# Splitting the attention values and probabilities: three float32r products per block in place of a native float32 one

## The chip, the cores and the metric

The kernel runs on one NeuronCore of a Trainium2 chip. The metric is the device time of one execution in microseconds; lower is better. Of the core's engines, PE is TensorE (matrix products), ACT is ScalarE, DVE is VectorE, POOL is GpSimd and SP is the queue that issues the transfers.

## The reference, cut to what matters

One layer of a decoder for 256 positions, all inputs and outputs float32. The part that the change touches is the attention of `nsa_attention`: eight heads in two groups, with a compressed, a selected and a window branch, each weighted by a gate:

```python
p_c = masked_softmax(s_c, mask_c)
o_c = jnp.einsum('bghqn,bngd->bqghd', p_c, vc)
...
p_s = masked_softmax(s_s, mask_s)
o_s = jnp.einsum('bghqm,bgqmd->bqghd', p_s, v_sel)
...
p_w = masked_softmax(s_w, mask_w)
o_w = jnp.einsum('bghqk,bkgd->bqghd', p_w, vwb)
return gbf[..., 0:1] * o_c + gbf[..., 1:2] * o_s + gbf[..., 2:3] * o_w
```

At 256 positions the selection takes every block, so the selected and the window branch are two causal attentions over all keys, w = 0 and 1, of different keys and values. Beside the attention runs an mLSTM of four heads, whose result `h` is normalised and gated; both branches are projected (`w_br`), merged by sigmoid gates of a projection `w_mg`, projected again, and followed by a gated MLP.

## The kernel before, in words

Weights stream in from HBM as float32 tiles `w`, issued on SP. For each weight tile ACT casts a high half `wh` to float32r (L154) and DVE subtracts a low half `wl` = `w` - `wh` (L157); a product of float32 accuracy then takes three float32r products (high by high, low by high, high by low). The helper `mm` (L112) issues them all. The moving operand is read through `turns`, which takes the two halves of its columns in turns. Four buffers hold `wh`, four `wl`, seven `w`. Where a text says fill, it means one `w_mg` tile: one `w`, `wh` and `wl`, and 12 products of 128x512 into `ps_mg`. DVE also multiplies rows of the adaLN weights with the conditioning vector (L276, "ada product"), 128x1024 each, which a ticker hands out one per weight tile. DVE's work thus comes in pairs of a `wl` and an ada product.

The stage in question lies at about 320 to 430 us. PE's order is written out by hand there, inside `tc.manual_schedule`; the order on ACT and DVE is set by the tile scheduler from the program's order, its dependencies and its own priorities, and each engine then works through its list in order. What the hand order says, in short (g is the group, t the half of the positions):

- `ml_weights` and `ml_num` make the mLSTM's numerators (`num`) from the values `mv1` that lie in `projA` behind the attention's values.
- `probs(g, t)` (`nsa_probs`) makes the probabilities: scores on PE, maxima on DVE, exponentials on ACT, then the gates over the sums (L987, L988), and the multiplication with them on DVE (L995) and ACT (L1003).
- `outs(g, t)` (`nsa_out`) goes over the blocks: t = 0 has two, t = 1 four, each 128 keys of one branch, and last the compressed one of 48 rows. For each block PE turns the probabilities of four heads over (L1019, into `ps_pT`), ACT copies them to `pT` (L947), and the block's product into `ps_y` follows one block later (`late`), with a fill between. At the end ACT and DVE split `ps_y` into the halves of `y_nsaT` (L1033, L1034).
- `ml_norm` normalises `num` beside outs(1, 0): DVE makes `vr` and `rs`, ACT does a square root (L205) and eight activations (L1083), DVE eight multiplications (L1085). `ml_outs` turns `num` over beside outs(1, 1) into `y_mlT` (L1097, L1098).
- Behind the last fill ACT takes eight sigmoids of `gates0` (L1171), and the products of `w_br` with `y_mlT` and `y_nsaT` begin (`ps_br`).

The window and selected products are native float32 (one instruction each, two records in the trace); the compressed one is float32r, since its values `vcm` and its `pT` already are. `behind(a, b)` makes the scheduler put a behind b on their engine, with no wait.

Of the kernel before, what the change touches and what calls it, by code (L numbers as in the profile page):

```python
# [14 lines left out]
P = 128  # L15
# [33 lines left out]
YA = 2  # L49
SLOW = (19,21,)  # L50
AHEAD, AHEADMOD, FIRST2 = {6: (11, 12), 7: (13,), 8: (15,), 9: (16,)}, 15, 3
ACOLS = 2596
AW = 392
A_MO, A_G, A_IF, A_V, A_MV = 0, 1024, 1048, 1056, 1568

# [25 lines left out]
def build(ctx: ExitStack, tc: tile.TileContext, d, out, dbg=None):  # L81
# [39 lines left out]
    def t2(shape, name, dt=F32):  # L121
        return p0.tile(shape, dt, name=name, tag="t2", bufs=NT2)
# [455 lines left out]
    KT = pa.tile([P, G, 2, 2, P], F32, name="KT")  # L578
    MV1 = MDV + 1
    projA = pa.tile([P, 2, ACOLS], F32, name="projA")  # L580
    mv1 = projA[:, :, A_MV:].rearrange("p t (h v) -> p t h v", v=MV1)
    nc.vector.memset(mv1[:, :, :, MDV:], 1.0)

    def conv():
# [205 lines left out]
    for gi, kn in enumerate(GROUPS):  # L790
        nxt = gi < len(GROUPS) - 1
        if nxt:
            for ks in STEPS[gi]:
                tk.add(ada_mod(k0 + kn + ks[0], k0 + kn + ks[-1] + 1))
        rate = None
        comp = []

        def work():
            if comp and next(comp[0], 1) is None:
                return  # L800
            comp.clear()
            pace = next(r for n, r in PACE if tiles[0] <= n)
            tk.tick((rate or pace) if nxt or c < 3 else GR2)
            if ring:
                tk.flush()

        c = 0
        first, lag = {}, []

        def catch_up():  # L810
            for args in lag:
                mm(*args)
            lag.clear()

        for b, ks in order_b(gi):
            j = b // 2
            if j not in psb:
                psb[j] = bank(psa if j < HELD else psm, "ps_b")
            ps = psb[j]
            whole = j < HELD  # L820
            shared = j < HELD + 4
            for k in ks:
                need(k0 + k)
                wh, wl = next(wb)
                o = ps[:, (b % 2) * S:(b % 2 + 1) * S]
                opening = k == 0 and (not shared or b % 2 == 0 and (not whole or gi == 0))
                new = first.setdefault(k, tiles[0]) == tiles[0]
                if tiles[0] <= 5:
                    continue
                end = k == kn - 1 and (not shared or b % 2 == 1 and not (whole and nxt))  # L830
                if not new:
                    catch_up()
                    mm_b(o, wh, wl, 0, hT, k0 + k, opening, end)
                else:
                    mm(o, wh, turns(hT[:, k0 + k, 0, :]), opening, False)
                    mm(o, wl, turns(hT[:, k0 + k, 0, :]), False, False)
                    lag.append((o, wh, turns(hT[:, k0 + k, 1, :]), False, end))
            if b % 2 == 1 and ks[-1] == kn - 1 and not (whole and nxt):
                catch_up()
                del psb[j]  # L840
                dst, src = dest_b(b // 2), ps.rearrange("p (a k t) -> p a t k", a=2, t=2)
                if gi == 0:
                    moved.append(lambda dst=dst, src=src: nc.scalar.copy(dst, src))
                elif whole:
                    nc.scalar.copy(dst, src)
                else:
                    ins = nc.vector.tensor_add(dst, src, dst)
                    if gi == 1 and b in SLOW:
                        slow.append(ins)
                if not nxt and b == 3:  # L850
                    ring.clear()
                    rate = GR1
                    comp.append(compress())
                    tk.add(ada_cols(3, 2, 0, KD))
                if not nxt and b == NBLK - 1:
                    conv()
        for c in range(6):
            pss = [bank(psm, "ps_a%d" % t) for t in range(2)]
            aw = AW if c < 4 else 512
            for k in range(k0, k0 + kn):  # L860
                need(k)
                wh, wl = next(wa if c < 4 else wv)
                if k or c:
                    for t in range(2):
                        mm_a(pss[t][:, :aw], hT, k, t, wh, wl, k == k0, k == k0 + kn - 1)
                else:
                    for x, w in ((0, wh), (1, wh), (0, wl)):
                        for t in range(2):
                            mm(pss[t][:, :aw], hT[:, k, x, t * P:(t + 1) * P], turns(w), not x and w is wh, False)
                if not nxt and c in (3, 4) and (k - k0) % 3 == 2:  # L870
                    next(steps)
            for t in range(2):
                dst, src = projA[:, t, c * AW:(c + 1) * AW], pss[t][:, :aw]
                if c >= 4:
                    dst = mv1[:, t, 2 * c - 8:2 * c - 6, :MDV]
                    src = src.rearrange("p (h v) -> p h v", v=MDV)
                if gi == 0:
                    moved.append(lambda dst=dst, src=src: nc.scalar.copy(dst, src))
                else:
                    nc.vector.tensor_add(dst, src, dst)  # L880
            if not nxt:
                if c == 2:
                    while comp:
                        work()
                    Pk = pa.tile([P, 16, 48], F32R, name="Pk", tag="c4")
                    nTr = pa.tile([36, 384], F32R, name="nTr", tag="xe")
                    steps = gate_steps(Pk, nTr)
                    next(steps)
        k0 += kn
# [42 lines left out]
    def fill(n, rate=RATES[0]):  # L932

        for _ in range(n):
            if next(filler, 1) is None:
                tk.tick(rate)


    y_nsaT = pg.tile([P, H, 2, S], F32R, name="y_nsaT", tag="u16")
    y_mlT = p0.tile([P, 8, 2, S], F32R, name="y_mlT", tag="t16")  # L940
    nev = [0]
    marks = {}

# [6 lines left out]
    def nsa_probs(g, t):  # L950
# [53 lines left out]
                                                          scale=l8[:, b, w:w + 1])  # L1004
        return Pt

    def nsa_out(g, t, Pt):
        psy = bank(psa, "ps_y")
        blocks = [(tt, w) for tt in range(t + 1) for w in range(2)] + [None]
        late = None  # L1010
        for i, blk in enumerate(blocks):
            n = P if blk else 48
            ps = bank(psa, "ps_pT")
            for hh in range(HPG):
                if blk is None:
                    src = Pk[:, t * H + g * HPG + hh, :].bitcast(F32)
                else:
                    src = Pt[hh // 2][:, hh % 2, blk[1], :] if t == 0 else Pt[hh][:, blk[0], blk[1], :]
                nc.tensor.transpose(ps[:n, hh * P:(hh + 1) * P], src, ident)  # L1019
            pT = t2([P, 512], "pT", F32 if blk else F32R)  # L1020
            ins = evac(pT[:n], ps[:n])
            if ins is not None:
                marks["last"] = ins
            if late is not None:
                late()
            v = vcm[:, g, :] if blk is None else projA[:, blk[0], A_V + (blk[1] * 2 + g) * P:
                                                       A_V + (blk[1] * 2 + g + 1) * P]
            late = lambda v=v, pT=pT, n=n, i=i: mm(psy, v, pT[:n], i == 0, i == len(blocks) - 1)
            yield
        late()  # L1030
        src = psy.rearrange("p (h k) -> p h k", h=HPG)
        hi = y_nsaT[:, g * HPG:(g + 1) * HPG, 0, t * P:(t + 1) * P]
        nc.scalar.copy(hi, src)  # L1033
        nc.vector.tensor_sub(y_nsaT[:, g * HPG:(g + 1) * HPG, 1, t * P:(t + 1) * P], src, hi)  # L1034


    stm = pa.tile([P, MH, 2, 6], F32, name="stm")
# [17 lines left out]
    def ml_num(h, W):  # L1055
        pn = [bank(psa, "ps_n") for _ in range(2)]
        mm(pn[0][:, :MV1], W[:, 0:P], mv1[:, 0, h], True, True)
        mm(pn[1][:, :MV1], W[:, P:2 * P], mv1[:, 0, h], True, False)
        mm(pn[1][:, :MV1], W[:, 2 * P:3 * P], mv1[:, 1, h], False, True)
        for t in range(2):  # L1060
            nc.scalar.copy(num[:, h, t], pn[t][:, :MDV])
            nc.vector.tensor_copy(den[:, t, h:h + 1], pn[t][:, MDV:MV1])
        for t in range(2):
            nc.vector.bn_stats(stm[:, h, t, :], num[:, h, t, :])
            nc.vector.bn_aggr(mvm[:, h, t, :], stm[:, h, t, :])
# [50 lines left out]
    with tc.manual_schedule(engines={mybir.EngineType.PE}):  # L1116
# [10 lines left out]
        for h in range(MH):  # L1127
            ml_num(h, Ws[h])
            if h % 2:
                fill(h // 2 + 1)  # L1130
        probs(0, 1)
        fill(3)
        outs(0, 0)
# [7 lines left out]
        outs(1, 0, norm)  # L1141
        run_all(norm)
        fill(2)
        outs(1, 1, ml_outs())
        fill(1)
        fill(8 * (NU0 + NU1))
# [651 lines left out]
```

## Time and profile before

| what | value |
|---|---|
| median of 3 runs | 1371.25 us (1370.47 to 1371.87) |
| the profiled execution | 1370.62 us |
| its span | 1368.8 us |
| granted TensorE clock | 1.00 |
| busy PE / DVE / ACT | 1349.4 / 1088.0 / 731.7 us |

The span runs from the first to the last instruction; the time of an execution has 1.8 us more. The lines of the profile stand in the prediction where they are used. In a row of the timeline come the start in us, the busy time, the engine, line and operation, the tiles written and read, and in brackets how long the engine sat idle before it and what ended that. In the chain come start, length and the instructions; a row of one tile's instructions has the shortest, middle and longest duration in ns.

### The profile page before, as it was taken

Reading aid. Unit: us, or ns where it says so; the run is one execution under the profiler, and the core shown is the slowest. Engines: PE = TensorE matmul, PEld = TensorE weight load, DVE = VectorE, ACT = ScalarE, POOL = GpSimd, SP = SyncE. Lnnn points to the kernel's source line nnn. Section 1 sums busy time; section 2 is a strip of 40 time slices with the busy share of each in tenths; the row PEclk is TensorE's granted clock in tenths of the full one; section 3 lists DMA queues with packets and bytes.
Section 4 is the critical chain, followed back from the end, with each engine's and each line's share of the span. In section 5 each row is a group of like instructions: output and inputs, shape, how many; then the busy total and the mean of one; then the engine's idle time right before and its main releaser. Section 6 shows DMA issues by size and latency. Waiting matters only on the chain.

```text
span 1368.8 us, 20928 instructions
## 1 busy us (share of the span) xinstructions
PE 1349.4 (99%) x7862; PEld 1203.5 (88%) x7862; DVE 1088.0 (79%) x1643; ACT 731.7 (53%) x1050; POOL 3.6 (0%) x11
## 2 busy tenths in 40 slices
PE   7999999999999999999999999999999999999998
PEld 6999998888778888889799999988889999998887
DVE  8899978998787897779899889865557667676568
ACT  7654455556576444445765555553345555555342
POOL 0000000000000000000000000000000000000000
PEclk9999999999999999999999999999999999999999
DMA  9999988996877998995389888866666666666662
GB/s 387 418 419 378 389 320 300 351 325 230 320 254 286 377 326 301 401 349 211 133 323 312 295 277 298 290 215 203 199 210 201 200 201 201 201 201 202 206 201 83
DMA packets 104181, 376.19 MB, mean 275 GB/s; under 512 B 11248, under 2 KB 11792, under 8 KB 103568
## 3 DMA queue, kind: packets, MB, share of 16 engines
q1 hardware_dynamic: 104080, 374.86, 77.8%
q8 instruction: 61, 1.00, 0.3%
q14 instruction: 40, 0.33, 0.1%
HBM read 372.70 MB, written 2.11 MB: 274 GB/s over the span
## 4 chain that ended last, share of the span: by engine, by line
PE 79%; DVE 10%; DMA 7%; ACT 2%; issue 2%; SPq 0%; DVEq 0%; ACTq 0%
PE ps_up L112 32%; PE ps_d L112 14%; PE ps_mg L112 11%; PE ps_br L112 6%; PE ps_b L112 4%; PE ps_a L112 4%; DVE wl L157 3%; PE ps_o L112 3%; DMA w<-in_w_in_b_dram 2%; PE ps_u L112 2%; DMA w<-in_w_in_a_dram 1%; PE ps_s L112 1%; PE ps_y L112 1%; ACT wh L154 1%; DVE w L276 1%
## 5 line engine op out<-in xcount | busy, mean ns | idle before, releaser
L154 ACT CAST wh<-w 128x1024 fp32r<-128x1024 f32 (+1 forms) x470 | 484.3, 1035 | 508.6 <-PE ps_up L112 145.2
L157 DVE TENSOR_TENSOR wl<-w,wh 128x1024 fp32r<-128x1024 f32 (+1 forms) x470 | 563.8, 1205 | 241.6 <-ACT wh L154 238.3
L112 PE MATMUL ps_up<-h2T,wh 128*128 128x512 f32 x1344 | 440.6, 382 | 0.0
L112 PE MATMUL ps_up<-h2T,wl 128*128 128x256 f32 x1344 | 366.3, 273 | 0.0
L112 PEld LDWEIGHTS ps_up<-h2T,wh 128*128 128x128 f32 x1344 | 253.9, 189 | 35.3
L112 PEld LDWEIGHTS ps_up<-h2T,wl 128*128 128x128 f32 x1344 | 258.0, 192 | 0.1
L112 PE MATMUL ps_d<-wh,uTt 128*128 128x512 f32 (+1 forms) x704 | 198.4, 366 | 0.0
L112 PE MATMUL ps_mg<-wh,hT 128*128 128x512 f32 x512 | 163.2, 389 | 0.0
L276 DVE SCALAR_TENSOR_TENSOR w<-w,crow 128x1024 f32<-128x1024 f32 x132 | 160.8, 1219 | 0.0
L112 PEld LDWEIGHTS ps_d<-wh,uTt 128*128 128x128 f32 x704 | 129.8, 189 | 16.6
L112 PE MATMUL ps_d<-wl,uTt 128*128 128x512 f32 (+1 forms) x352 | 128.8, 366 | 0.0
L112 PE MATMUL ps_b<-hT,wh 128*128 128x256 f32 x768 | 124.4, 276 | 4.2 <-ACT hT L437 3.2
L112 PEld LDWEIGHTS ps_b<-hT,wh 128*128 128x128 f32 x768 | 111.0, 192 | 6.0 <-ACT hT L437 3.8
L112 PEld LDWEIGHTS ps_mg<-wh,hT 128*128 128x128 f32 x512 | 96.8, 189 | 16.0 <-issue 3.1
L112 PE MATMUL ps_a<-wh,hT 128*128 128x392 f32 (+1 forms) x384 | 102.9, 347 | 0.5 <-ACT wh L154 0.5
L112 PE MATMUL ps_mg<-wl,hT 128*128 128x512 f32 x256 | 97.2, 380 | 0.5 <-DVE wl L157 0.5
L112 PE MATMUL ps_b<-hT,wl 128*128 128x256 f32 x384 | 90.7, 275 | 0.0
L112 PEld LDWEIGHTS ps_d<-wl,uTt 128*128 128x128 f32 x352 | 66.7, 189 | 8.2
L112 PEld LDWEIGHTS ps_a<-wh,hT 128*128 128x128 f32 x384 | 69.3, 189 | 4.9 <-ACT wh L154 0.9
L112 PE MATMUL ps_a<-wl,hT 128*128 128x392 f32 (+1 forms) x192 | 67.4, 352 | 2.2 <-DVE wl L157 2.1
L112 PEld LDWEIGHTS ps_b<-hT,wl 128*128 128x128 f32 x384 | 67.5, 192 | 0.1
L112 PE MATMUL ps_o<-wh,mgT 128*128 128x512 f32 x192 | 57.6, 380 | 0.0
(324 smaller groups left out, 1404.3 us busy)
## 6 DMA issues: line engine op xcount, KB each, us to landing
w<-in_w_up_dram SPq DMA_DIRECT2D x176, 512.0 KB, 4.3
w<-in_w_ada_dram SPq DMA_DIRECT2D x132, 512.0 KB, 5.1
w<-in_w_down_dram SPq DMA_DIRECT2D x89, 512.0 KB, 4.2
w<-in_w_mg_dram SPq DMA_DIRECT2D x64, 512.0 KB, 5.4
w<-in_w_in_b_dram SPq DMA_DIRECT2D x48, 512.0 KB, 10.5
w<-in_w_br_dram SPq DMA_DIRECT2D x32, 512.0 KB, 5.2
w<-in_w_o_dram SPq DMA_DIRECT2D x32, 512.0 KB, 5.2
adaA<-in_w_ada_dram SPq DMA_DIRECT2D x15, 1024.0 KB, 10.6
```

What stands on the lines that cost most here:

```text
L112: ins = nc.tensor.matmul(o, lhsT, rhs, start=start, stop=stop)
L154: hi = nc.scalar.copy(wh[:, :n], t[:, :n])
L157: lows.append(nc.vector.tensor_sub(wl[:, :n], t[:, :n], wh[:, :n]))
L276: ins = nc.vector.scalar_tensor_tensor(t, t, 1.0, crow[:, i * 1024:(i + 1) * 1024], op0=ALU.mult, op1=ALU.mult, accum_out=parts[:, row(m), ...
```

## The change

The projections' tile `projA` is cut to 1568 columns, and the mLSTM's values `mv1` get a tile of their own. Once `ml_num` has read them for the last time, a tile `vq` takes that place: two slots for the low halves of probabilities and two for the high and low half of group 1's values. Group 0's values go to `vp`, in the place where `y_mlT` will lie, which is made only ahead of outs(1, 1). `split_values` fills them with two ACT casts and two DVE subtractions. In `nsa_out`, `pT` becomes float32r for all blocks (ACT casts where it copied), DVE subtracts a low half `pL` from `ps_pT` for each window or selected block, and three products (low value by high probability, high by high, high value by low probability) in turns replace the native one. The compressed product reads its `pT` in turns too. Since the columns come out in turns, `ps_y` is read back with its heads in another order.

```diff
@@ -49,7 +49,7 @@
 YA = 2
 SLOW = (19,21,)
 AHEAD, AHEADMOD, FIRST2 = {6: (11, 12), 7: (13,), 8: (15,), 9: (16,)}, 15, 3
-ACOLS = 2596
+ACOLS = 1568
 AW = 392
 A_MO, A_G, A_IF, A_V, A_MV = 0, 1024, 1048, 1056, 1568
 
@@ -578,7 +578,7 @@
     KT = pa.tile([P, G, 2, 2, P], F32, name="KT")
     MV1 = MDV + 1
     projA = pa.tile([P, 2, ACOLS], F32, name="projA")
-    mv1 = projA[:, :, A_MV:].rearrange("p t (h v) -> p t h v", v=MV1)
+    mv1 = pa.tile([P, 2, MH, MV1], F32, name="mv1", tag="mv1")
     nc.vector.memset(mv1[:, :, :, MDV:], 1.0)
 
     def conv():
@@ -870,8 +870,10 @@
                 if not nxt and c in (3, 4) and (k - k0) % 3 == 2:
                     next(steps)
             for t in range(2):
-                dst, src = projA[:, t, c * AW:(c + 1) * AW], pss[t][:, :aw]
-                if c >= 4:
+                src = pss[t][:, :aw]
+                if c < 4:
+                    dst = projA[:, t, c * AW:(c + 1) * AW]
+                else:
                     dst = mv1[:, t, 2 * c - 8:2 * c - 6, :MDV]
                     src = src.rearrange("p (h v) -> p h v", v=MDV)
                 if gi == 0:
@@ -937,7 +939,6 @@
 
 
     y_nsaT = pg.tile([P, H, 2, S], F32R, name="y_nsaT", tag="u16")
-    y_mlT = p0.tile([P, 8, 2, S], F32R, name="y_mlT", tag="t16")
     nev = [0]
     marks = {}
 
@@ -1004,6 +1005,18 @@
                                                           scale=l8[:, b, w:w + 1])
         return Pt
 
+    vparts, spare, nlow = [], [], [0]
+
+    def split_values():
+        spare.append(pa.tile([P, 4, 512], F32R, name="vq", tag="mv1"))
+        vparts.append(p0.tile([P, 2, 512], F32R, name="vp", tag="t16"))
+        vparts.append(spare[0][:, 2:4, :])
+        for g in range(2):
+            raw = projA[:, :, A_V:A_V + 512].rearrange("p t (w g x) -> p t w g x", w=2, g=2)[:, :, :, g]
+            hi, lo = [vparts[g][:, x].rearrange("p (t w x) -> p t w x", t=2, w=2) for x in range(2)]
+            behind(nc.scalar.copy(hi, raw), marks["num"])
+            nc.vector.tensor_sub(lo, raw, hi)
+
     def nsa_out(g, t, Pt):
         psy = bank(psa, "ps_y")
         blocks = [(tt, w) for tt in range(t + 1) for w in range(2)] + [None]
@@ -1017,21 +1030,32 @@
                 else:
                     src = Pt[hh // 2][:, hh % 2, blk[1], :] if t == 0 else Pt[hh][:, blk[0], blk[1], :]
                 nc.tensor.transpose(ps[:n, hh * P:(hh + 1) * P], src, ident)
-            pT = t2([P, 512], "pT", F32 if blk else F32R)
+            pT = t2([P, 512], "pT", F32R)
             ins = evac(pT[:n], ps[:n])
             if ins is not None:
                 marks["last"] = ins
+            if blk is None:
+                parts = [(vcm[:, g, :], turns(pT[:n]))]
+            else:
+                pL = spare[0][:, nlow[0] % 2, :]
+                nlow[0] += 1
+                nc.vector.tensor_sub(pL, ps, pT)
+                b = 2 * blk[0] + blk[1]
+                h, l = [vparts[g][:, x, b * P:(b + 1) * P] for x in range(2)]
+                parts = [(l, turns(pT)), (h, turns(pT)), (h, turns(pL))]
             if late is not None:
                 late()
-            v = vcm[:, g, :] if blk is None else projA[:, blk[0], A_V + (blk[1] * 2 + g) * P:
-                                                       A_V + (blk[1] * 2 + g + 1) * P]
-            late = lambda v=v, pT=pT, n=n, i=i: mm(psy, v, pT[:n], i == 0, i == len(blocks) - 1)
+
+            def late(parts=parts, i=i):
+                for j, (v, p) in enumerate(parts):
+                    mm(psy, v, p, i == 0 and j == 0, i == len(blocks) - 1)
             yield
         late()
-        src = psy.rearrange("p (h k) -> p h k", h=HPG)
-        hi = y_nsaT[:, g * HPG:(g + 1) * HPG, 0, t * P:(t + 1) * P]
+        src = psy.rearrange("p (h k a) -> p a h k", h=HPG // 2, a=2)
+        hi, lo = [y_nsaT[:, g * HPG:(g + 1) * HPG, x, t * P:(t + 1) * P].rearrange("p (a h) k -> p a h k", a=2)
+                  for x in range(2)]
         nc.scalar.copy(hi, src)
-        nc.vector.tensor_sub(y_nsaT[:, g * HPG:(g + 1) * HPG, 1, t * P:(t + 1) * P], src, hi)
+        nc.vector.tensor_sub(lo, src, hi)
 
 
     stm = pa.tile([P, MH, 2, 6], F32, name="stm")
@@ -1058,7 +1082,7 @@
         mm(pn[1][:, :MV1], W[:, P:2 * P], mv1[:, 0, h], True, False)
         mm(pn[1][:, :MV1], W[:, 2 * P:3 * P], mv1[:, 1, h], False, True)
         for t in range(2):
-            nc.scalar.copy(num[:, h, t], pn[t][:, :MDV])
+            marks["num"] = nc.scalar.copy(num[:, h, t], pn[t][:, :MDV])
             nc.vector.tensor_copy(den[:, t, h:h + 1], pn[t][:, MDV:MV1])
         for t in range(2):
             nc.vector.bn_stats(stm[:, h, t, :], num[:, h, t, :])
@@ -1128,6 +1152,7 @@
             ml_num(h, Ws[h])
             if h % 2:
                 fill(h // 2 + 1)
+        split_values()
         probs(0, 1)
         fill(3)
         outs(0, 0)
@@ -1141,6 +1166,7 @@
         outs(1, 0, norm)
         run_all(norm)
         fill(2)
+        y_mlT = p0.tile([P, 8, 2, S], F32R, name="y_mlT", tag="t16")
         outs(1, 1, ml_outs())
         fill(1)
         fill(8 * (NU0 + NU1))
```

The scheduler puts the new and old instructions of DVE and ACT in another order. On DVE, from the reciprocal of the first outs on (`l8` is the sum's reciprocal, `pt` the probabilities, `parts` the sums of the ada products), before:

```order
L987 RECIPROCAL l8_3509<-l8_3509 128x8
L988 TENSOR_TENSOR l8_3509<-l8_3509,gsig_445 128x8
L995 TENSOR_TENSOR pt_3514<-pt_3514,l8_3509 128x512
L995 TENSOR_TENSOR pt_3530<-pt_3530,l8_3509 128x512
L157 TENSOR_TENSOR wl_3658<-w_3655,wh_3657 128x1024
L276 SCALAR_TENSOR_TENSOR w_3645,parts_75<-w_3645,crow_82 128x1024
L157 TENSOR_TENSOR wl_3687<-w_3684,wh_3686 128x1024
L276 SCALAR_TENSOR_TENSOR w_3674,parts_75<-w_3674,crow_82 128x1024
L157 TENSOR_TENSOR wl_3744<-w_3741,wh_3743 128x1024
L276 SCALAR_TENSOR_TENSOR w_3703,parts_75<-w_3703,crow_82 128x1024
L157 TENSOR_TENSOR wl_3765<-w_3762,wh_3764 128x1024
```

and with the change, at the same place, where `vq_3509` written from `ps_pT` is the low half of the first block:

```order
L157 TENSOR_TENSOR wl_3668<-w_3665,wh_3667 128x1024
L276 SCALAR_TENSOR_TENSOR w_3652,parts_75<-w_3652,crow_82 128x1024
L988 RECIPROCAL l8_3515<-l8_3515 128x8
L989 TENSOR_TENSOR l8_3515<-l8_3515,gsig_446 128x8
L996 TENSOR_TENSOR pt_3520<-pt_3520,l8_3515 128x512
L996 TENSOR_TENSOR pt_3536<-pt_3536,l8_3515 128x512
L157 TENSOR_TENSOR wl_3699<-w_3696,wh_3698 128x1024
L276 SCALAR_TENSOR_TENSOR w_3684,parts_75<-w_3684,crow_82 128x1024
L157 TENSOR_TENSOR wl_3756<-w_3753,wh_3755 128x1024
L276 SCALAR_TENSOR_TENSOR w_3715,parts_75<-w_3715,crow_82 128x1024
L1042 TENSOR_TENSOR vq_3509<-ps_pT_3621,pT_3626 128x512
L157 TENSOR_TENSOR wl_3777<-w_3774,wh_3776 128x1024
```

One pair has moved ahead of the reciprocal; the low half stands behind the two pairs that follow the multiplications. On DVE in outs(1, 0), with the change, from the multiplications to the second low half (`rs_ml` leads to `vr`):

```order
L996 TENSOR_TENSOR pt_4001<-pt_4001,l8_3980 128x512
L157 TENSOR_TENSOR wl_4167<-w_4164,wh_4166 128x1024
L276 SCALAR_TENSOR_TENSOR w_4148,parts_75<-w_4148,crow_82 128x1024
L157 TENSOR_TENSOR wl_4199<-w_4196,wh_4198 128x1024
L276 SCALAR_TENSOR_TENSOR w_4183,parts_75<-w_4183,crow_82 128x1024
L1042 TENSOR_TENSOR vq_3509<-ps_pT_4065,pT_4070 128x512
L210 RECIPROCAL rs_ml_4080<-rs_ml_4080 128x8
L157 TENSOR_TENSOR wl_4220<-w_4217,wh_4219 128x1024
L276 SCALAR_TENSOR_TENSOR w_4215,parts_75<-w_4215,crow_82 128x1024
L1042 TENSOR_TENSOR vq_3509<-ps_pT_4114,pT_4119 128x512
L215 TENSOR_TENSOR rs_ml_4080<-rs_ml_4080 128x8
```

Two pairs stand ahead of the first low half here, and a further pair and the second low half between L210 and the rest of the chain to `vr`. On ACT in outs(1, 0), before:

```order
L947 COPY pT_4094<-ps_pT_4089 128x512
L154 CAST wh_4218<-w_4216 128x1024
L947 CAST pT_4127<-ps_pT_4122 48x512
L926 COPY gates0_3086<-ps_mg0_3880 128x512
L926 COPY gates0_3086<-ps_mg1_3881 128x512
L154 CAST wh_4256<-w_4254 128x1024
L1033 CAST y_nsaT_3087<-ps_y_4040 128x4x128
L1083 ACTIVATE num_3393<-num_3393,vr_4051,rs2_4052 128x256 x8
L154 CAST wh_4294<-w_4292 128x1024
```

and with the change:

```order
L948 CAST pT_4119<-ps_pT_4114 128x512
L1107 ACTIVATE num_3393<-num_3393,vr_4076,rs2_4077 128x256 x8
L154 CAST wh_4250<-w_4248 128x1024
L948 CAST pT_4155<-ps_pT_4150 48x512
L928 COPY gates0_3087<-ps_mg0_3902 128x512
L928 COPY gates0_3087<-ps_mg1_3903 128x512
L154 CAST wh_4291<-w_4289 128x1024
L1057 CAST y_nsaT_3088<-ps_y_4064 128x4x128
```

The eight activations have moved ahead of the compressed block's pT and of a `wh` cast. On ACT at the end of the stage, with the change:

```order
L154 CAST wh_4512<-w_4510 128x1024
L948 CAST pT_4397<-ps_pT_4392 48x512
L1197 ACT_TABLE_LOAD
L1197 ACTIVATE gates0_3087<-gates0_3087 128x512 x8
L1121 ACTIVATE y_mlT_4238<-ps_yT_4402,prm_70 128x256
L154 CAST wh_4533<-w_4531 128x1024
```

Before, the cast that now opens this piece stood behind the sigmoids. On PE and SP nothing else has moved beside the products themselves, but for a few `w_br` products at the end of the stage.

## The prediction

> **What bounds the kernel now.** I read the page's busy shares and its chain first, then the stage that the change touches.
>
> ```profile
> PE 1349.4 (99%) x7862; PEld 1203.5 (88%) x7862; DVE 1088.0 (79%) x1643; ACT 731.7 (53%) x1050; POOL 3.6 (0%) x11
> PE 79%; DVE 10%; DMA 7%; ACT 2%; issue 2%; SPq 0%; DVEq 0%; ACTq 0%
> PEclk9999999999999999999999999999999999999999
> ```
>
> and of the windows of 20 us in that stage (busy PE, weight loads, DVE, ACT, POOL, then the clock) the one with the least PE:
>
> ```profile
> 380.00:400.00 20.00, 19.67 (x92) 15.80 (x91) 15.65 (x33) 16.24 (x36) 0.00 (x0) 1.00 0.70 251
> ```
>
> PE (TensorE) works 99% of the span and carries 79% of the chain: PE time saved or lost anywhere should show at the end, if nothing later takes it up. That window has PE at 19.67 of 20 us, DVE at 15.65, ACT at 16.24, and a granted clock of 1.00. There is no slack on PE; on DVE and ACT there is some, but both work through their queues in order, so what counts is what stands ahead of a new instruction. The chain of the stage, in order of time (start, us), and the rows of ps_y:
>
> ```profile
> 338.62 0.44 PE ps_pT L1019 x4
> 339.06 0.86 PE ps_y L112 x2
> 339.92 2.59 PE ps_mg L112 x12
> ...
> 357.86 0.86 PE ps_y L112 x2
> ...
> 389.05 1.12 PE ps_y L112 x2
> ...
> 396.65 0.43 PE ps_y L112
> ```
>
> ```profile
> L112 PE MATMUL ps_y<-pT,projA x24: 592/594/697, 338.9 to 419.6; 128*128 128x512 f32 x24
> L112 PE MATMUL ps_y<-pT,vcm x4: 491/495/502, 346.3 to 425.1; 48*128 48x512 f32 x4
> L1034 DVE TENSOR_TENSOR y_nsaT<-ps_y,y_nsaT x4: 681/686/687, 350.4 to 429.6; 128x512 fp32r<-128x512 f32 x4
> ```
>
> Twelve blocks cost two records each: 0.86 us of PE per native product (the 389.05 one is 1.12, since it waited 0.26 for pT). A compressed product takes 0.43. A ps_mg product, float32r with its moving operand read in turns, takes 2.59/12 = 0.216.
>
> **The products.** A block goes from 0.86 to 3 x 0.216 = 0.65, so 12 x 0.21 = 2.55 us less PE. The four compressed products now read in turns too: 4 x (0.42 - 0.22) = 0.8. If the turns do nothing for 48 rows the second is 0; I take 0.8, since ps_mg has the same moving length. Together -3.4.
>
> **Splitting the values.** Two ACT casts and two DVE subtractions of 128x512, of the kind of the y_nsaT rows (0.69, pitch 0.60). They stand ahead of probs(0,1) on engines with gaps, so PE pays nothing itself; DVE runs about 1.2 us later for some microseconds, which counts below. The strided reading of psy adds between 0 and one more 0.69 off the path: 0. mv1's own place and the later y_mlT move no work: 0.
>
> **The low halves.** Each block needs a DVE subtraction (0.69) before its third product, where only ACT's pT was needed. The rows show where DVE is then:
>
> ```profile
> 332.89 0.20 DVE L987 RECIPROCAL l<-l 128x8 f32<-128x8 f32 x1 [2.83 <-ACT pt L984]
> 333.33 1.29 DVE L995 TENSOR_TENSOR pt<-pt,l 128x512 f32<-128x512 f32 x2
> ...
> 339.10 1.22 DVE L157 TENSOR_TENSOR wl<-w,wh 128x1024 fp32r<-128x1024 f32 x1
> 340.24 1.22 DVE L276 SCALAR_TENSOR_TENSOR w<-w,crow 128x1024 f32<-128x1024 f32 x1
> ...
> 359.05 0.08 DVE L276 DVE_READ_ACCUMULATOR w<-w,crow 128x1 f32 x1
> ...
> 390.14 1.22 DVE L276 SCALAR_TENSOR_TENSOR w<-w,crow 128x1024 f32<-128x1024 f32 x1
> 391.29 0.20 DVE L210 RECIPROCAL rs_ml<-rs_ml 128x8 f32<-128x8 f32 x1
> ```
>
> DVE takes a wl and an ada product in pairs, 2.28 us a pair. In the first block of each outs the order puts the low half behind such pairs. All times below are in the clock of before, each outs for itself:
> - outs(0,0): one pair has moved into the 2.83 us gap, but DVE starts about 1 us later and two pairs still stand between the L996 multiplies and the low half. The second pair's wl waits for its cast (337.17 + 1.09 in the rows of ACT further on), so the low half ends at 341.0 to 341.4. The third product is due at 339.06 + 0.43 = 339.5: PE waits 1.8.
> - outs(0,1): behind the pair that ends at 359.05 to 359.1, so 359.8 against 357.86 + 0.43 = 358.3: 1.5.
> - outs(1,0): behind the pair that ends at 391.29, so 392.0. The third product ends at 392.2, where the native one ended at 389.05 + 1.12 = 390.2: 2.0 later, that is a wait of 2.2 beyond the gain of 0.2.
> - outs(1,1): behind four pairs that start with the cast behind the normalisation, at 401.2 (next part). Four pairs are 9.1, a y_nsaT low half 0.6 and its own 0.65: 411.6. PE, released at 401.6, has the compressed product and two fills (5.4), transposes, a fill and transposes (3.5) and two products (0.4) ahead: 410.9. I take 0.75, between 0.3 and 1.2.
>
> Later blocks have a 2.59 fill and 0.44 of transposes between them, 3.0 us for one pair and a subtraction (2.28 + 0.60): no wait, or 0.1. Every wait lets PE's followers stand too, but nothing comes back to it: the casts that the next pairs need are themselves released by PE, as the row at 351.84 below shows.
>
> **The normalisation on ACT.** The change also turns the order of two pieces of ACT:
>
> ```profile
> 337.17 1.09 ACT L154 CAST wh<-w 128x1024 fp32r<-128x1024 f32 x1
> ...
> 351.84 1.05 ACT L154 CAST wh<-w 128x1024 fp32r<-128x1024 f32 x1 [3.87 <-PE ps_mg L112]
> ...
> 390.31 0.30 ACT L205 ACTIVATE rs_ml<-vr,epsc 128x8 f32<-128x8 f32 x1
> ...
> 393.76 0.57 ACT L947 CAST pT<-ps_pT 48x512 fp32r<-48x512 f32 x1
> ...
> 398.60 4.05 ACT L1083 ACTIVATE num<-num,vr,rs 128x256 f32<-128x256 f32 x8
> ...
> 420.45 1.28 ACT L1171 ACT_TABLE_LOAD   x1
> 421.75 4.27 ACT L1171 ACTIVATE gates<-gates 128x512 f32<-128x512 f32 x8
> ```
>
> Before, the compressed block's pT (393.76) stood ahead of the eight num activations (398.60); now it and a wh cast stand behind them. They wait for vr, which DVE makes behind L210 (392.2 now), a pair, the second low half and five operations on 128x8 like the RECIPROCAL rows (0.20): 392.2 + 2.3 + 0.65 + 1.0 = 396.1. Then 4.05 for the eight, 1.0 for the cast and 0.57 for pT: 401.6. PE, 1.8 late by then (2.0 - 0.2), is due at 396.65 + 1.8 = 398.45, so it waits 3.1. The bounds: 0 if vr is ready at 393, 4 if DVE's pair is held by its cast.
>
> The longest wait of PE that shows its clock here is that of these rows:
>
> ```profile
> 15.03 0.44 PE L410 MATMUL ps_nT<-head,xt 128*128 128x128 f32 x2 [1.45 <-ACT xt L401]
> 18.67 1.16 PE L112 MATMUL ps_b<-hT,wh 128*128 128x256 f32 x8 [1.80 <-ACT hT L437]
> ```
>
> After 1.80 us idle the granted clock stayed at full in the page's row. [...]
>
> **The tail.** Before the last compressed product ACT now has a wh cast ahead of pT, the table load and the eight sigmoids (1.28 + 4.27, rows above). That cast takes the buffer which PE leaves only at the end of a fill; call this time T. pT is ready at T + 1.6, when PE needs it; table and sigmoids end at T + 7.15, the last y_mlT at T + 7.6, the next wh at T + 8.6, its wl at T + 9.8. PE has 8 products, the compressed one, 12 and 16 products before it needs them, (36 x 0.216 + 0.2) = T + 8.0, and the wl half a microsecond later: 1.4 to 1.8, I take 1.6. At least 0, if the cast finds another buffer.
>
> **The sum.** -3.4 + 1.8 + 1.5 + 2.2 + 3.1 + 0.75 + 1.6 = +7.55. From w_br on PE is followed by all engines and nothing waits for an absolute time for long, so the lag stays: I take back 0. The profiled execution took 1370.62 (span 1368.8 and 1.8 around it), 0.63 below the median of 1371.25. So 1378.2 against the one and 1378.8 against the other: 1378.5. A measurement of this kernel can tell 0.2% (2.74 us) from no change: under 1368.5 is faster, over 1374.0 slower.
>
> **Rivals.**
> 1. *Faster: the low halves come in time.* If DVE ran 2 to 3 us earlier at the four places than I laid out, because the pairs slip into idle time (2.83 us ahead of the reciprocal, and 4.35 us of 20 in the window row), every wait but the ones on ACT's own order would vanish, and vr would be ready at 393, which takes the 3.1 as well. From 2.2 us earlier it decides; then -3.4 and 1367.9, at most +1.6 with the tail. Against it: the printed DVE order, in which the pairs stand ahead. 0.08.
> 2. *Waits overlap.* If the wl pairs and casts follow their DMAs rather than PE, DVE and ACT keep their old times while PE falls behind, and the waits don't add up: only the latest counts, pT at 401.6 against 396.65, +5.0, less the gains after it (1.2), and no tail wait: about +3.5, 1375. If vr also comes 2 us sooner, +1.5 to 2.5, 1373.3. For it: DVE's idle time; against it the 3.87 us in which ACT waited for PE. 0.17 for the two together, 0.10 of them within 0.2%.
> 3. *The clock drops.* [...] 0.08.
> 4. *The turned products are no faster than 0.42.* Twelve blocks would cost 3 x 0.42 = 1.27 instead of 0.65, +7.4, and 1386. Against it: 0.216 in ps_mg. 0.03.
>
> **How the numbers follow.** My forecast has 0.64, its own range 1375.5 to 1381.0 from the bounds of the waits (first blocks each 0.4 either way, the num wait 2.5 to 4, the tail 0 to 1.8). The range 1373.0 to 1383.0 adds most of the second rival and the third, and leaves out the first, the fourth and some of the second. Faster 0.08; within 0.2%: 0.12, the second's 0.10 and a little of the first; slower 0.80.
>
> **What would show it.** Right: idle rows of PE ahead of ps_y with DVE's subtraction (L1042) as releaser in the first block of each outs, about 1.8, 1.5, 2.2 and 0.75; one of about 3 us with ACT pT as releaser before the compressed product of outs(1,0); ps_y products 0.216 apart; PE in w_br 1.6 behind ACT's sigmoids; the lag unchanged from 440 us to the end. Wrong: a first ps_y group of three without a wait, nums that start before 394 us, a granted clock under 1.00 near 400 us, or a wait further on that shrinks by what PE lost here.

## The result and the profile after

The changed kernel takes 1380.33 us (median of 6 runs, 1378.26 to 1384.74) against 1370.92 us (6 runs): a ratio of 1.0073, with a 95% interval of 1.0058 to 1.0087. The ratios in this document are worked out over all runs; the two medians alone would give 1.0069. The profiled execution took 1378.26 us, 7.64 more than the profiled one of before; it is the fastest of the six. Two lines of its page follow (the second is the chain that ended last), then the waits of PE from 300 to 450 us (us in total, times, longest), and one window of 20 us (length, busy time and instructions of PE, PEld, DVE, ACT and POOL, then the granted clock, the DMA share and GB/s); PEld is TensorE's loading of weights:

```profile
PE 1350.8 (98%) x7874; PEld 1207.7 (88%) x7874; DVE 1096.7 (80%) x1657; ACT 732.3 (53%) x1052; POOL 3.6 (0%) x11
PE 79%; DVE 10%; DMA 5%; ACT 3%; issue 3%; SPq 0%; DVEq 0%; ACTq 0%
```

```profile
PE ps_y L112 <- DVE vq L1042: 5.9, 4, 2.3
PE ps_y L112 <- ACT pT L948: 1.5, 3, 1.0
```

```profile
380.00:400.00 20.00, 17.40 (x72) 13.18 (x71) 16.17 (x34) 12.24 (x30) 0.00 (x0) 0.91 0.68 234
```

Before, PE stood still for 0.3 us in the whole stage. Now it waits 5.9 for low halves and 1.5 for pT, and the granted clock of the window from 380 to 400 falls from 1.00 to 0.91. The timeline of PE shows where, and DVE's what stood ahead of the first low half:

```profile
341.70 0.48 PE L112 MATMUL ps_y<-vq,vp 128*128 128x512 f32 x1 [1.82 <-DVE vq L1042]
...
361.82 0.48 PE L112 MATMUL ps_y<-vq,vp 128*128 128x512 f32 x1 [1.50 <-DVE vq L1042]
...
395.31 0.79 PE L112 MATMUL ps_y<-vq 128*128 128x512 f32 x1 [2.28 <-DVE vq L1042]
395.90 0.63 PE L112 MATMUL ps_mg<-wh,hT 128*128 128x512 f32 x1
...
404.64 0.48 PE L112 MATMUL ps_y<-pT,vcm 48*128 48x512 f32 x1 [0.99 <-ACT pT L948]
...
414.73 0.48 PE L112 MATMUL ps_y<-vq 128*128 128x512 f32 x1 [0.33 <-DVE vq L1042]
```

```profile
339.81 1.22 DVE L276 SCALAR_TENSOR_TENSOR w<-w,crow 128x1024 f32<-128x1024 f32 x1
340.96 0.08 DVE L276 DVE_READ_ACCUMULATOR w<-w,crow 128x1 f32 x1
340.96 0.69 DVE L1042 TENSOR_TENSOR vq<-ps_pT,pT 128x512 fp32r<-128x512 f32 x1
```

Laid side by side, product by product, the two traces give PE's lag behind the kernel before. It is worked out for the fills of each part as the difference of the starts of the same products: -0.1 us at 330 us, +2.0 after outs(0,0), +3.3 after outs(0,1), +7.0 at the second block of outs(1,0), +8.0 after its compressed product, +7.8 at 450, 7.7 at 600 and 7.8 at the end. All of the loss is made between 338 and 410 us.

### The profile page after: what moved, and what is told of

Same layout as the page of the kernel before. It is cut to its first block, busy times and chain, and to the rows that moved or that the text cites. A ratio compares the mean times of both kernels' runs of the same rounds, so it can differ in the third digit from the quotient of the medians.

```text
span 1376.4 us, 20961 instructions
## 1 busy us (share of the span) xinstructions
PE 1350.8 (98%) x7874; PEld 1207.7 (88%) x7874; DVE 1096.7 (80%) x1657; ACT 732.3 (53%) x1052; POOL 3.6 (0%) x11
## 4 chain that ended last, share of the span: by engine, by line
PE 79%; DVE 10%; DMA 5%; ACT 3%; issue 3%; SPq 0%; DVEq 0%; ACTq 0%
PE ps_up L112 32%; PE ps_d L112 17%; PE ps_mg L112 9%; PE ps_br L112 6%; PE ps_b L112 5%; DVE wl L157 3%; PE ps_a L112 3%; PE ps_o L112 3%; PE ps_u L112 2%; DVE w L276 2%; DMA w<-in_w_in_a_dram 1%; ACT wh L154 1%; PE ps_s L112 1%; DMA w<-in_w_in_b_dram 1%; DMA w<-in_w_mg_dram 1%
```

## The experiments

Two theories stood against each other. A: the loss is the sum of PE's waits for operands that stand behind pairs in DVE's queue or behind the num activations in ACT's, with what a wait brings with it. B: DVE and ACT are too full in this stage, and waits taken away at one place come back at others.

**The first low halves ahead (e1_low_first).** `gate` holds the low half's subtraction, and the fourth `wl` after it is put behind it:

```diff
+        if gate:
+            gate[1] -= 1
+            if not gate[1]:
+                behind(lows[-1], gate[0])
+                gate.clear()
...
-                nc.vector.tensor_sub(pL, ps, pT)
+                ins = nc.vector.tensor_sub(pL, ps, pT)
+                if i == 0:
+                    gate[:] = [ins, 4]
```

> The change with one thing moved on DVE: in the first block of each outs the low half of the probabilities stands ahead of the wl and ada pair of the fourth fill after it, not behind it (this also puts the eight num activations behind the compressed block's pT on ACT). Theory A, the lag is the sum of the waits for the low half and for that pT, each with a restart of about 0.27 us of PE behind it, and of the slower clock that the longest wait brings: idle PE ahead of the first blocks' third product falls from 1.8, 1.5, 2.3 and 0.3 to at most 0.3 each, the granted clock stays at 1.00 from 380 to 420 us, and what is left is the products' gain of 2.6 less about 1: 1 to 2 us under the kernel before, 1369 to 1370. Rival B, the waits are only the visible end of a DVE and ACT that are too busy: the waits move to other products or to wl, and the time falls by 2 us at most, to 1377 to 1379.

Measured: 1375.84 us against 1370.72, a ratio of 1.0034 (1.0022 to 1.0047). That is about half of the loss, between the theories. PE's waits from 300 to 450 us of this kernel, and from its timeline the first of the long ones, in the second block of outs(0,0):

```profile
PE ps_y L112 <- DVE vq L1048: 4.9, 5, 1.3
PE ps_y L112 <- ACT pT L954: 0.5, 2, 0.3
```

```profile
345.10 0.48 PE L112 MATMUL ps_y<-vq,vp 128*128 128x512 f32 x1 [1.22 <-DVE vq L1048]
```

The first blocks' long waits are gone, but the second blocks of the first three outs now wait 1.1 to 1.3 each: their low halves stand behind two pairs, where one had stood. No wait passes 1.3, and four of five runs have a mean clock of 1.000.

**The num activations back in their place (e2_num_back).** In `ml_norm` two `yield`s, and each of the eight put behind the compressed block's pT:

```diff
+        yield
+        yield
+        late = [marks["last"]]
...
-                nc.scalar.activation(num[:, h, t, :], num[:, h, t, :], AF.Identity,
-                                     bias=vr[:, t, h:h + 1], scale=rs[:, t, h:h + 1])
+                ins = nc.scalar.activation(num[:, h, t, :], num[:, h, t, :], AF.Identity,
+                                           bias=vr[:, t, h:h + 1], scale=rs[:, t, h:h + 1])
+                behind(ins, late[0])
```

> The change with the eight num activations put back behind the compressed block's pT on ACT, and nothing else. Theory A: the wait of 1.0 for that pT and its restart go, the other waits and the slower clock stay: 1.3 us less than the change, 1378.5 to 1379.5 by the medians. Rival, the forecast's own size of this wait (3.1): up to 3 us less, 1377. Rival B: no change, since PE waits for something else at the same place.

Measured: 1382.62 us (4 runs), a ratio of 1.0083 (1.0069 to 1.0096), no gain over the change. The wait of 0.99 is gone, and further on its timeline shows a longer one; the windows of 2 us around it follow:

```profile
414.19 0.48 PE L112 MATMUL ps_y<-vq 128*128 128x512 f32 x1 [2.27 <-DVE vq L1042]
```

```profile
412.00:414.00 2.00, 0.00 (x0) 0.00 (x0) 2.00 (x4) 0.62 (x2) 0.00 (x0) 1.00 1.03 358
414.00:416.00 2.00, 1.81 (x8) 1.58 (x9) 2.00 (x3) 0.48 (x1) 0.00 (x0) 0.70 0.91 336
416.00:418.00 2.00, 2.00 (x6) 1.60 (x5) 1.46 (x5) 0.47 (x1) 0.00 (x0) 0.50 1.01 397
```

PE arrives earlier at outs(1,1) (its lag at 404 us is 5.6 in place of 8.0), where DVE's pairs had not got further, and waits there; the clock then goes to half (0.50 from 416 to 418 us). At this place theory B was right. The lag is 8.9 at 450 us, against 7.8 with the change. Another 2.9 of this profile's loss come at 660 to 690 us, far behind the edit, where PE waits 2.1 for the normalisation ahead of the MLP and the clock halves again (0.85 from 668 to 672 us and 0.72 from 672 to 676).

**The third product one fill later (e4_low_later).**

```diff
             def late(parts=parts, i=i):
-                for j, (v, p) in enumerate(parts):
+                if low:
+                    mm(psy, *low.pop(), False, False)
+                for j, (v, p) in enumerate(parts[:2]):
                     mm(psy, v, p, i == 0 and j == 0, i == len(blocks) - 1)
+                low.extend(parts[2:])
```

> The change with the third product of each block (high value by low probability) issued one fill later on PE, together with the next block's first two; the same instructions otherwise. Theory A: no wait for a low half is left, the clock stays at 1.00, and the products' gain of 2.6 shows nearly whole: 2 to 2.6 us under the kernel before, 1368.3 to 1369. Rival B: DVE is too busy to deliver the low halves, waits of 1 us and more remain, 1374 or more.

Measured: 1392.08 us, a ratio of 1.0146 (1.0132 to 1.0160). The experiment was ill made. With two places for low halves, block i's product now comes after the subtraction of block i+2 into the same place; so it read the wrong block's low half, and waited for it (timeline):

```profile
365.31 0.80 PE L112 MATMUL ps_y<-vq,vp 128*128 128x512 f32 x1 [4.23 <-DVE vq L1042]
```

In outs(0,0), with two blocks only, no wait was left. The form with four places is e9 below.

**The compressed product straight (e5_vcm_plain).** Its columns then go to the wrong heads; only the time counts here.

```diff
-                parts = [(vcm[:, g, :], turns(pT[:n]))]
+                parts = [(vcm[:, g, :], pT[:n])]
```

> The change with the compressed product reading pT straight and not in turns, so that its columns are added to the wrong heads. If the turns gained nothing there (0.41 against 0.42 us by the chains), the compressed product stays at 0.41 to 0.43 and the time is that of the change within its scatter, 1378 to 1382; if the turns are what makes 0.41, it rises above 0.5.

Measured: 1381.56 us (one run). The four products last 494 to 499 ns against 480 in turns, and on the chain 0.42 to 0.43 against 0.41. The turns gain 0.01 us there, not 0.2. In this execution the fill behind the very first wait took 4.28 us in place of 2.59 (chain), with a granted clock of 0.50 from 344 to 346 us:

```profile
342.62 0.48 PE ps_y L112
343.11 4.28 PE ps_mg L112 x12
```

**All low halves ahead (e6_low_all)**, as e1 with a list of gates, one for every block; **no wait for a low half (e8_no_low_wait)**, where the third product reads what ACT has made; and **one wait put back (e7_one_wait)**, e6 with e2's edit and without the gate of the first block of outs(1,0). The three in this order:

```diff
-                nc.vector.tensor_sub(pL, ps, pT)
+                gates.append([nc.vector.tensor_sub(pL, ps, pT), 4])
```

```diff
-                parts = [(l, turns(pT)), (h, turns(pT)), (h, turns(pL))]
+                parts = [(l, turns(pT)), (h, turns(pT)), (h, turns(pT))]
```

```diff
+                ins = nc.vector.tensor_sub(pL, ps, pT)
+                if (g, t, i) != (1, 0, 0):
+                    gates.append([ins, 4])
```

> The change with the low half of every block put ahead of the wl and ada pair of the fourth fill after it on DVE, not only that of the first blocks; the eight num activations stand behind the compressed block's pT on ACT. Theory A: the waits of 1.1 to 1.3 that the first version of this left ahead of the second blocks' third products go too, only the two short waits for pT (0.2 and 0.3, each with a restart of about 0.27) stay, the clock stays at 1.00, and the products' gain of 2.6 shows but for them: 1.5 to 2.3 us under the kernel before. Rival B, DVE has too much to do in this stage: the waits go to still later blocks or to wl, and it stays 2 us or more slower than the kernel before.

> The change with the third product of each block reading pT in place of the low half, so that the low probabilities are left out; DVE still makes the low halves, and PE has the same number of products, but none waits for DVE. Theory A: the waits for the low half are the whole loss, so this ends where the version with all low halves ahead ends, 1.5 to 2.3 us under the kernel before. Rival B: DVE's added work delays wl and so PE all the same, 1372 to 1376. Rival C, the split products themselves cost more than the native one: slower than the kernel before although no wait is left.

> As the version with all low halves ahead, but the first block of outs(1,0) keeps its low half behind the pair, as in the change, with the num activations held behind the compressed block's pT. Theory A: one wait of 2.3 and its restart come back, and in a part of the runs the clock falls to half for about 3.4 us behind it, 1.7 us more: 2.5 to 4.5 us above that version, with a granted clock of 0.997 to 0.999 in the runs and a larger scatter. Rival: the wait is taken up later, since DVE and ACT get ahead meanwhile, and the time differs by less than 1 us.

Measured, each over 11 runs against the same runs of before: e6 1370.74 us, 1.0001 (0.9992 to 1.0010); e8 1371.30, 1.0000 (0.9991 to 1.0009); e7 1373.50, 1.0013 (1.0004 to 1.0022). e6 and e8 agree, as A says, and lie level with the kernel before: with the same products on PE and the same subtractions on DVE, the loss goes when the long waits go. That they are level and not 2 us faster is not what A said. The waits that are left, first in e6, then in e8:

```profile
PE ps_y L112 <- ACT pT L953: 0.5, 2, 0.3
PE ps_y L112 <- DVE vq L1047: 0.5, 1, 0.5
```

```profile
PE ps_y L112 <- ACT pT L948: 1.0, 3, 0.4
PE ps_yT L1116 <- DVE vq L1042: 0.7, 1, 0.7
```

From 342 to 376 us PE's lag in e6 falls by 0.21 with every block and by 0.02 with a compressed product, as it should; but the short waits, each with a start of PE behind it (about 0.27, worked out further on), give it back. The lag steps up by 0.55 at the first block, 0.1 at the first of outs(1,0), and by 0.6 twice in outs(1,1), each beside a gain of 0.2.

e7 puts one wait of 2.28 back. Of its eleven runs the four with a mean clock of 1.000 took 1371.11 to 1371.32 us, the seven with 0.997 to 0.999 took 1373.49 to 1374.50. In the profiled one, of the second kind, the product behind the wait and its fill took from 392.07 to 396.66, 4.59 us, against 2.91 behind the first wait of the change (341.70 to 344.61): the slower clock (0.57 from 392 to 396 us, against 1.00 there) costs 1.7. The rest of the price stays open. The profiled run ends 3.15 behind e6's, which leaves about 1.5 for the wait itself, but the four runs at full clock lie only 0.4 to 0.6 above e6's median, and none of them was profiled; the 2.2 to 3.4 between the two groups are more than the clock's 1.7. A mean clock by itself tells little: 18 of the 27 runs of the kernel before show 0.998 or 0.999 too.

**A version with the waits avoided (e9_deferred, e9a_low_vr).** e9: e4 with four places (two more in `vp`), in all outs but outs(1,1); low halves of group 1 ahead of a pair; `vr` put ahead in the same way. e9a: e6 with the `vr` edit, and with the first low half of outs(1,1) one `wl` earlier, as in e9.

```diff
-        vparts.append(p0.tile([P, 2, 512], F32R, name="vp", tag="t16"))
+        vparts.append(p0.tile([P, 4, 512], F32R, name="vp", tag="t16"))
...
-                pL = spare[0][:, nlow[0] % 2, :]
+                pL = lowslots[nlow[0] % (2 if g and t else 4)]
...
+                if g:
+                    gates.append([ins, 3 if i == 0 and t else 4])
...
+                if not (g and t):
+                    low.extend(parts[2:])
...
-        nc.vector.scalar_tensor_tensor(vr, rs, -1.0, mvm[:, :, :, 0].rearrange("p h t -> p t h"),
-                                       op0=ALU.mult, op1=ALU.mult)
+        gates.append([nc.vector.scalar_tensor_tensor(vr, rs, -1.0, mvm[:, :, :, 0].rearrange("p h t -> p t h"),
+                                                     op0=ALU.mult, op1=ALU.mult), 6])
```

> The change with the third product one fill later on PE in three of the four outs, with four places for low halves instead of two (two more beside group 0's values), the low halves of group 1's outs ahead of a pair on DVE, and vr ahead of the next pair. Theory A: the version with all low halves ahead stayed level because four short waits of 0.2 to 0.5 (two for pT, two for low halves in outs(1,1)), each with a restart, cost 2.4 of the gain of 2.6; here the one in outs(1,1) and the late low half of outs(0,0) go, so 1 to 2 us under the kernel before, a ratio of 0.9985 to 0.9993. It also says that the first version with a later third product was slow (1392) only for want of places: no wait of 4 us is left. Rival: a later third product is slow by itself, 1375 or more.

> As the version with all low halves ahead, and vr ahead of the next pair on DVE, and the first low half of outs(1,1) a pair earlier; the third product stays at its place. Theory A: the two short waits in outs(1,1) go or shrink, about 1 us less than that version: 0.5 to 1.5 us under the kernel before. Rival: the eight num activations now stand ahead of a gates copy on ACT and take as much back: level with the kernel before.

Measured: e9 1371.09 us, 1.0004 (0.9995 to 1.0013); e9a 1372.11 us, 1.0008 (0.9999 to 1.0017). Theory A's time missed in both; e9a came out level, as its rival said. In e9 the lag does reach -1.4 us at 405, and no wait of 4 us is left, so a later third product is not slow by itself. But it is back at +0.2 by 420: outs(1,1), where four low halves and the mLSTM's outputs share DVE and ACT, takes it all. In e9a PE waits 1.1 for a `wh` cast there. PE's waits in e9 from 300 to 450 us:

```profile
PE ps_yT L1129 <- DVE y_mlT L1135: 0.9, 1, 0.9
PE ps_y L112 <- ACT pT L954: 0.5, 2, 0.3
PE ps_y L112 <- DVE vq L1049: 0.3, 1, 0.3
```

**Three of the four outs (e10_three_of_four).** e9, but outs(1,1) keeps the native products.

```diff
+            elif g and t:
+                parts = [(projA[:, blk[0], A_V + (blk[1] * 2 + g) * P:A_V + (blk[1] * 2 + g + 1) * P], pT)]
```

> As the version with the third product one fill later in three outs, but outs(1,1) keeps the native float32 products, unturned, as before the change: eight blocks are split, four are not, and no low half is made beside the mLSTM's outputs. Theory A: the lag of about -1.5 us which that version had reached at 405 us lasts, since what took it back were waits inside outs(1,1) on an ACT and DVE that had four low halves more: 1 to 1.7 us under the kernel before, a ratio of 0.9988 to 0.9993. Rival: the loss does not come from the low halves of outs(1,1) but from the later num activations, and the time is level with the kernel before.

Measured: 1370.16 us against 1371.22 (11 and 15 runs), a ratio of 0.9989 (0.9980 to 0.9998): about 0.1% under the kernel before, with an interval that only just leaves out no change. Theory A holds here: the lag is -1.4 at 405 us and still -1.4 at 450, and two short waits are left:

```profile
PE ps_y L112 <- ACT pT L954: 0.5, 2, 0.3
```

Some of it is taken back at 660 us, where in the profiled execution the normalisation ahead of the MLP keeps PE for 1.7 us, 1.2 more than before.

## Why the prediction came out as it did

The direction, the time (1378.5 against 1380.33, inside the range) and the main mechanism were right: PE waits where DVE's queue holds the low half back, and the lag stays. The sum of +7.55 agrees with the 7.64 of the two profiled executions, but partly because errors cancel, which is luck. Of the signs that the prediction named, the idle rows in the first block of each outs, the products 0.216 apart and the lasting lag came; the wait of about 3 us for pT and the `w_br` products 1.6 behind the sigmoids did not; and one of its signs of being wrong came, a granted clock under 1.00 near 400 us (0.68 from 396 to 400).

- *The waits for the first low halves*: 1.8, 1.5, 2.2 and 0.75 were forecast, 1.82, 1.50, 2.28 and 0.33 measured. DVE's queue, read in the printed order with durations of before, told the first three to a tenth. Missing was what comes behind a wait: on the chain the product that had waited takes 0.48, not 0.216, so each wait costs 0.27 more. Missing too were short waits, 0.21 for pT in the first block and about 0.3 in the last one of outs(0,1).
- *The num activations*: 3.1 was forecast, 0.99 measured, and yet outs(1,0) as a whole came out as laid out: the lag rose by 4.75 (3.29 to 8.04), against 2.0 - 0.2 + 3.1 - 0.2 = 4.7 (the last is the gain forecast for the compressed product). ACT set its end, as forecast:

```profile
399.13 4.05 ACT L1107 ACTIVATE num<-num,vr,rs 128x256 f32<-128x256 f32 x8 [3.81 <-DVE vr L1101]
403.08 1.03 ACT L154 CAST wh<-w 128x1024 fp32r<-128x1024 f32 x1
404.02 0.57 ACT L948 CAST pT<-ps_pT 48x512 fp32r<-48x512 f32 x1
```

  pT ends at 404.6, which less the lag of 3.3 is 401.3 in the clock of before (forecast 401.6). PE came later than forecast, since it had lost 1.6 to the slower clock (the waiting product and its fill took 4.50, from 395.31 to 399.81, against 2.91 behind the first wait) and 0.3 to the start behind the wait, and so waited less. What PE loses ahead of an end that ACT sets comes out of its wait; the right 4.75 is no proof of the 3.1.
- *The products*: 0.21 per block as forecast; the compressed product's 0.8 was mis-sized: 0.04 (0.41 against 0.42 four times). The row nearest to it was its own, not ps_mg.
- *The tail*: 1.6 was forecast and none came. I counted 8 products between the cast and the compressed product; there is a whole fill and more:

```profile
429.14 1.05 ACT L154 CAST wh<-w 128x1024 fp32r<-128x1024 f32 x1 [1.17 <-issue]
430.09 0.57 ACT L948 CAST pT<-ps_pT 48x512 fp32r<-48x512 f32 x1
```

  pT was ready at 430.7, and PE took it at 434.8. So +0.8 for the compressed product and about +1.3 for starts and short waits stand against -1.6 for the tail and -0.4 in outs(1,1).
- *That the lag stays* was right: 7.8 at 450 us and at the end.
- *The second rival*, that waits overlap, held in part: in outs(1,0) as told above, and in e2, which took the num wait away and got a longer one in outs(1,1).
- *The third rival*, the clock, got 0.08 and came about: behind the wait of 2.28 the clock was at 0.50 for 3.41 us (395.15 to 398.56), which cost 1.6. The profile of before, with a clock of 1.00 from 7 to 1368 us, shows no drop from which the price of this rival, and the part of the range that stands for it, could be worked out. The prediction had seen the clock stay full after 1.80 us of idle PE at 18.67 us; in the profile of the change the same 1.80 stands at 18.48 us, and there the clock is 0.50 from 19.68 to 23.09 us. Of the six runs the two slowest (1382.04 and 1384.74 us) have the two lowest mean clocks, 0.995 and 0.994; the other three that took longer than the profiled one show its 0.997, so what made them 1.3 to 2.3 us longer is open.

## What to carry to other kernels

Here an operand that had to pass a second engine cost what stood ahead of it in that engine's queue (waits of 1.82, 1.50 and 2.28 us), not only its own 0.6 us (340.96 to 341.56 in the change): read the built order of that engine, find the first consumer after each pause, and lay the durations end to end. The gain of 0.2 us per block was smaller than the price of one short wait on this saturated PE (in e6 the lag still rose by 0.55 at the first), so split only where the side engines have room, and consume the late operand one step later. Where two waits lie in a row, taking the first away may only feed the second (in e2 the 0.99 went, and 2.27 came behind it).

## What was not expected of the hardware

The granted clock fell to half behind idle times of PE of about 2 us (1.80 at 18.48 us and 2.28 at 395.31 in the change). In the profile of the change, windows of 4 us:

```profile
388.00:392.00 4.00, 4.00 (x23) 3.30 (x21) 3.57 (x6) 4.00 (x9) 0.00 (x0) 1.00 0.00 0
392.00:396.00 4.00, 1.40 (x5) 0.90 (x5) 4.00 (x8) 3.29 (x5) 0.00 (x0) 0.89 0.91 296
396.00:400.00 4.00, 4.00 (x15) 3.18 (x14) 3.19 (x10) 0.87 (x2) 0.00 (x0) 0.68 1.05 368
400.00:404.00 4.00, 3.65 (x19) 2.88 (x17) 3.16 (x8) 4.00 (x8) 0.00 (x0) 1.00 0.31 127
```

The two waits there are 0.32 and 2.28, with 0.7 us of products between. In e5 a wait of 0.21 and one of 1.82 did the same (0.50 from 344 to 346 us), where the same pair of waits left the change's own profile at full clock (1.00 from 340 to 344). In windows of 4 us over the whole span the change, e2, e4, e5 and e7 show drops to half clock ahead of the kernel's last 10 us, and before and e10 show none. The two of the change last 3.41 us each (19.68 to 23.09 and 395.15 to 398.56); by the shares of their windows those of e2, e5 and e7 last 3.4, and of the four in e4 two last 3.4 and two 6.9. The two starts in the change are 375.47 us apart, 110 times 3.413; by the same shares the starts are 395.9 and 256.0 apart in e2 (116 and 75 times), 324.3 and 54.6 in e5 (95 and 16 times), and 344.7, 10.2 and 54.6 in e4 (101, 3 and 16 times). Counted from the drops in stretches of this length, the same two waits of 0.32 and 2.28 fall into one stretch in the change, and into two in e2. The first two of these windows are of the change, the other three of e2:

```profile
391.73:395.15 3.42, 0.98 (x5) 0.34 (x3) 3.42 (x6) 3.39 (x6) 0.00 (x0) 1.00 0.82 248
395.15:398.56 3.41, 3.25 (x8) 2.59 (x9) 3.34 (x9) 0.16 (x1) 0.00 (x0) 0.50 1.01 384
```

```profile
390.91:394.33 3.42, 1.97 (x10) 1.18 (x8) 3.42 (x5) 3.39 (x7) 0.00 (x0) 1.00 0.49 164
394.33:397.74 3.41, 2.26 (x10) 2.01 (x11) 3.41 (x8) 1.15 (x2) 0.00 (x0) 1.00 0.95 278
397.74:401.15 3.41, 3.41 (x19) 2.95 (x18) 2.86 (x10) 2.56 (x5) 0.00 (x0) 1.00 1.01 404
```

With PE busy for 0.98 us of a stretch the next one is at half clock; with 1.97 and 2.26 it is not. The pair of 0.21 and 1.82 likewise lies within one stretch in e5 (PE busy for 1.50) and across two in the change (2.55 and 2.25). Before and the change, from 10 us on and ahead of their last 10, and the part of this stage in the timelines of e2, e4 and e5 hold nine more stretches at full clock with less than 2 us of busy PE. Four have a drop right behind them: 1.60 (the change, from 16.27 us), 1.14 (e2, from 411.39), and 0.66 and 1.22 (e4, from 360.43 and 370.67). Five have none: 1.59 and 1.92 (e2, from 339.71 and 360.19), 1.96 (the change, from 12.86), and 1.83 and 1.93 (before, from 13.77 and 17.19); busy time is the profile's, in which the ends of products are modelled. So here it was not the length of a wait alone that decided: the same two waits brought a drop in the change and none in e2. How little PE worked in the stretch that they fell into fits all of these but for the two of 1.59 and 1.60, which came out differently. How the stretches lie differs between profiled executions: the first drop starts at 19.68 us in the change, at 18.9 in e2 and at 19.1 in e4 and e5. That e7's runs fall into two groups would fit this. With waits up to 1.3 (e1) the granted clock is 1.00 in every window of 20 us from 300 to 460, and four of five runs stayed at 1.000.
